# RWKV-7 time mixing on one core: where the k and r mixes are split, who makes the key norms' reciprocals, and which queue asks for the up weights

## The chip, the cores and the metric

The kernel runs on one core of a Trainium2 chip. The metric is the device time of one execution in microseconds (us). Before the change three runs gave 1647.22 us as median (1646.68 to 1648.98). One further execution was recorded by the profiler.

## What is computed

The reference is one layer of RWKV-7 time mixing with a residual, for 2048 tokens of width 1024 in 16 heads of 64. Each token's normalised input `h` is mixed with that of the token before it, once for each projection:

```python
dx = token_shift(h) - h
x_r, x_w, x_k, x_v, x_a, x_g = (h + dx * mu[i] for i in range(6))
r = x_r @ w_r;  k = x_k @ w_k;  v = x_v @ w_v;  g = silu(x_g @ w_g)
w_lo = tanh(x_w @ w_lo_w);  a_lo = x_a @ w_lo_a
decay = exp(-exp(-softplus(-(w0 + w_lo @ w_up)) - 0.5));  a = sigmoid(a0 + a_lo @ a_up)
kk = normalised per head (k * k_k);  k = k * (1 + (a - 1) * k_a)
# per token and head: S = S * decay + (S @ -kk) (kk * a)^T + v k^T;  y = S r
y = group_norm(y) + sum(r * k * r_k) * v
out = x + (y * g) @ w_out
```

All of it is in float32.

## The kernel before

A product of two float32 matrices is made of three matmuls. Each factor is split into a high part (the value rounded to the matmul's own 32-bit format, `fp32r`) and a low part (what is left), and the three products high x high, high x low and low x high are summed in PSUM. `split` (line 95) does this: ScalarE copies the value into the high part, another engine, VectorE as a rule, subtracts that from the value to get the low part. So each mix and each weight costs one ScalarE copy and one subtraction before TensorE can use it.

The work has three stages. The tokens are cut into 8 blocks of 256 (`NB`, index `b`), the width into 8 slices of 128 (`NCT`, index `ct`).

The first stage (lines 542 to 653, up to 477 us) runs over the blocks. For each slice it loads the input, makes `h` and `dx`, feeds the low-rank product `lps`, and makes four mixes. The mix for v goes into the tiles `mixa` (high and low) and the one for g into `mixb`; both are split there. The mixes for k and r (`mok`, `mor`, tag `mo`) are stored to DRAM unsplit, in `mkr_d`. In block 0 ScalarE and GpSimd make those two, in the others VectorE does. Then come the v product (two groups of columns by two groups of 128 tokens, so four PSUM sums, with three PSUM buffers of the tag `vg`) and the g product (eight sums over the same three buffers). `mixa` and `mixb` exist once, so a slice of them is written for the next block only when the product of this block has read it. The tiles `x`, `h`, `dx` and `mo` have two buffers each. In this stage a scheduler lays out the order of all engines' instructions from its own estimates; the order is then fixed.

The second stage (lines 655 to 1078, 477 to 1142 us) has an order written out by hand (`manual_schedule`) for TensorE, VectorE, ScalarE and GpSimd. `first_k` makes the k product of block 0. Then `step(b, p)` runs for each block and each of eight groups of 128 columns (`p`): it makes the r product of block `b` (`r_proj`, from `mixa`) and the k product of block `b + 1` (`k_proj`, from `mixb`), and the elementwise chains around them (`chain_a`, `chain_b`, `chain_c`). The mixes come back from DRAM by `load_mix`: the k mixes of block `b + 2` are asked for at `p == 6`, when `mixb` has been read, the r mixes of block `b + 1` at the end of `p == 7`. `load_mix` loads the raw mix into the low tile and returns eight steps, each of which splits one slice; `take(mixes, ...)` puts the steps into the order at `p == 7` and at `p == 0`. Every second subtraction goes to GpSimd.

Three more things of this stage matter here. The key norms: `rs_a` (at `p == 7`) turns sums of squares into reciprocal roots by `rsqrt` (line 99), eleven small instructions on VectorE; `rs_b` (at the next `p == 0`, after one `k_proj`) transposes the result on TensorE (`ssp<-consts,rsk`). The up weights: `load_up(p + 1)` asks for the next 128 KB of `up_d` on SyncE's queue, right after the matmuls of `chain_a` (tile `wa`) have read the single buffer `up`. And the queue: nearly all DMAs are issued by SyncE (SP), in the order in which they stand, each after the waits of the one before it.

The last block's step (`last`) and the third stage (from line 1190, 1142 us on) run the recurrence over chunks of 32 tokens with the output projection; none of the edited lines is there. The weights `w_out` pass through two of the `mkr_d` buffers in the meantime (`wo_d`).

Of the kernel before, what the change touches and what calls it, by code (L numbers as in the profile page):

```python
# [39 lines left out]
def rwkv7_kernel(ctx, tc, a, T):  # L40
# [45 lines left out]
    up_d = dram.tile([NP, P, 2, P], F32, name="up_d")  # L86
    mkr_d = [dram.tile([P, 2, NCT, TB], F32, name=f"mkr_d{b}") for b in range(NB)]
    bn_d = [dram.tile([2, P, HEADS], F32, name=f"bn_d{b}") for b in range(NB)]

    wo_d = lambda p: mkr_d[2 + p // 4].rearrange("p k c t -> p (k c t)")[:, p % 4 * D : p % 4 * D + D]  # L90
    pl_d = [dram.tile([P, NC, NP], F32, name=f"pl_d{b}") for b in range(NB)]
# [6 lines left out]

    def rsqrt(pool, out, x, shape, nm):

        y = pool.tile(shape, F32, name=nm + "y", tag="rq", bufs=3)
        t = pool.tile(shape, F32, name=nm + "t", tag="rq", bufs=3)
        h = pool.tile(shape, F32, name=nm + "h", tag="rq", bufs=3)
        ts(y.bitcast(I32), x.bitcast(I32), -0.5, 1597463007.0, mul, add)
        ts(h, x, -0.5, None, mul)
        for it in range(3):
            tt(t, y, y, mul)
            tt(t, t, h, mul)
            stt(y if it < 2 else out, t, 1.5, y, add, mul)

# [65 lines left out]

    def load_mix(k, mix, b, pool=False, n=NCT // 2):

        hi, lo = mix
        for x in range(0, NCT, n):  # L180
            nc.sync.dma_start(lo[:, x : x + n].bitcast(F32), mkr_d[b][:, k, x : x + n])

        def step(x):
            raw = lo[:, x].bitcast(F32)
            nc.scalar.copy(hi[:, x], raw)
            (nc.gpsimd if pool and x % 2 else nc.vector).tensor_tensor(out=lo[:, x], in0=raw, in1=hi[:, x].bitcast(F32), op=sub)  # L186

        return [lambda x=x: step(x) for x in range(NCT)]

# [314 lines left out]
    with ExitStack() as p0:  # L504
# [37 lines left out]
        with ExitStack() as pa:  # L542
# [48 lines left out]
            for b in range(NB):  # L591
                (mvh, mvl), (mgh, mgl) = mixa, mixb
                lps = pps.tile([P, TB], F32, name=f"lps{b}", tag="lps", bufs=1)
                for ct in range(NCT):
# [12 lines left out]
                    for i, nm in enumerate("kr"):  # L607
                        mo = hp.tile([P, TB], F32, name=f"mo{nm}{b}{ct}", tag="mo")
                        if b == 0:
                            act(mo, dx, AF.Copy, scale=pr("mu_" + nm, ct))  # L610
                            nc.gpsimd.tensor_tensor(out=mo, in0=mo, in1=h, op=add)
                        else:
                            stt(mo, dx, pr("mu_" + nm, ct), h, mul, add)
                        nc.sync.dma_start(mkr_d[b][:, i, ct], mo)
                    stt(dx, dx, pr("mu_g", ct), h, mul, add)
# [29 lines left out]
                if b == NB - 1:  # L645
                    wk, steps = load_w(a["w_k"], "wk", stage)
                    do(steps)
                    do(load_mix(0, mixa, 0))
                for i in range(NCT):
# [5 lines left out]
        with ExitStack() as pb:  # L655
# [73 lines left out]
            def rs_a(b):  # L729
                tr = tokenmajor(st["ssc"], st["ss", b])  # L730
                ss = sm.tile([P, 2, 16], F32, name=f"ss{b}", tag="ss", bufs=2)
                with urgent():
                    ts(ss.rearrange("p q (j x) -> p q j x", x=4), tr, 2.0, 2e-24, mul, ALU.max)
                    rs = sm.tile([P, 2, 16], F32, name=f"rsk{b}", tag="ss", bufs=2)
                    rsqrt(sm, rs, ss, [P, 2, 16], f"rk{b}")
                st["rs", b] = rs
# [46 lines left out]
            def load_up(p):  # L783
                up = sm.tile([P, 2, P], F32R, name=f"up{p}", tag="up")
                st.setdefault("up", deque()).append(up)
                nc.sync.dma_start(up.bitcast(F32), up_d[p % NP])

            def chain_a(b, p):
# [10 lines left out]
                for j in range(2):  # L799
                    nc.tensor.matmul(wup[j], up[:, j], x[:, j], start=True, stop=False)  # L800
                    nc.tensor.matmul(wup[j], up[:, j], x[:, 2 + j], start=False, stop=True)  # L801
                load_up(p + 1)
                th = t_("th")
                act(th, wup[0], AF.Tanh, scale=0.5, bias=dprm[:, 0, p : p + 1])
                act(th, th, AF.Identity, scale=C, bias=cb)
                yield
                nc.vector.tensor_tensor_scan(th, rmask.rearrange("p c l -> p (c l)"), th, 0.0, mul, add)
# [127 lines left out]
            def step(b, p):  # L935
# [21 lines left out]
                if p == 2 and b > 0:  # L957
                    bn_out(b - 1)
                if first:
                    take(mixes, 3 if b else 0)  # L960
                else:
                    take(inv, INA[p])
# [5 lines left out]
                if first:  # L968
                    rs_b(b)
                    prod_t()  # L970
                    take(mixes, NCT)
                    k_next()
# [23 lines left out]
                if final:  # L996
                    rs_a(b + 1)
                    take(mixes, 0 if last_mix else NCT)
                else:
                    next(ga, None)  # L1000
                    next(ga, None)
                if p == 6:
                    if b + 2 < NB:
                        mixes.extend(load_mix(0, mixb, b + 2, True))
                    else:
                        mixes.extend(load_mix(1, mixb, NB - 1, True))
                if not final:
# [26 lines left out]
            def first_k():  # L1034

                for p in range(NP):
# [4 lines left out]
                    next(kn[0], None)  # L1041
                    take(mixes, NCT // 4)
                    do(st["wr"], p / NP, (p + 1) / NP)
# [4 lines left out]
                st["ssc"] = save(st["ss", 0], 0, "ss")  # L1048
                mixes.extend(load_mix(1, mixa, 0, True))
                ga = chain_a(0, 0)  # L1050
# [5 lines left out]
            with tc.manual_schedule(engines=MANUAL):  # L1056
                mixes = deque(load_mix(0, mixb, 1, True))
                load_up(0)
# [17 lines left out]
                def last():  # L1076
# [6 lines left out]
                    load_c(2)  # L1083
                    take(mixes, NCT)
                    for _ in range(3):
# [238 lines left out]
```

## Time and profile before

| | |
|---|---|
| median of three runs | 1647.22 us |
| the profiled execution | 1646.02 us, span in the profile 1644.2 us |
| granted TensorE clock, mean | 0.978 of 2.4 GHz |
| busy: TensorE, VectorE, ScalarE, GpSimd | 1507.0, 1190.7, 835.9, 358.0 us |
| TensorE in the first stage, 82 to 477 us | busy for 387.99 of 395 us |
| DMA | 269.03 MB, mean 164 GB/s |

An engine's busy time is the union of its instructions. A matmul's end is modelled and overlaps the start of the next, so what TensorE really issues is read from the distance between starts. In a list of waits, "idle" is the time just before an instruction, and the name behind the arrow is what ended it. PE is TensorE, DVE VectorE, ACT ScalarE, POOL GpSimd, SP SyncE, and SPq its DMA queue.

### The profile page before, as it was taken

The page shows a single profiled execution, that of the slowest core. Times are in us where ns is not written, and L with a number is a line of the kernel's source. Part 1 is how long each engine was busy: PE and PEld are TensorE (multiplying, and loading weights), DVE is VectorE, ACT ScalarE, POOL GpSimd, SP SyncE. Part 2 cuts the span into 40 slices and gives each one's busy share as a digit, 9 for nine tenths or more (in the row PEclk, how much of TensorE's full clock was granted, in tenths as well). Part 3 has the DMA queues.
Part 4 walks back from the last instruction along what each step waited for, and adds up shares of the span by engine and source line. Part 5 has one row for each costly group of instructions (what it writes and reads, how often), then busy time and mean ns, then how long its engine had stood idle before and what let it go on. Part 6 is the DMA issues. An engine that isn't in the chain of part 4 may idle for free. (4 is left out here: it accounts for less than half of the span.)

```text
span 1644.2 us, 46239 instructions
## 1 busy us (share of the span) xinstructions
PE 1507.0 (92%) x17776; PEld 1304.6 (79%) x17776; DVE 1190.7 (72%) x2900; ACT 835.9 (51%) x2126; POOL 358.0 (22%) x729
## 2 busy tenths in 40 slices
PE   3699999999989999989998989698899999999998
PEld 2589889999888888878787878687677787777776
DVE  7976776668655579787878778578568867876654
ACT  5653332223356455454546454477566666666551
POOL 4600000000002232222313232312233222323221
PEclk9899999999999999999999999799899999999999
DMA  5783433334574565556576666778866687677642
GB/s 178 223 263 126 145 119 112 127 126 154 149 224 113 139 138 152 120 151 151 148 160 159 139 168 150 205 205 238 203 184 177 184 193 205 179 189 185 177 108 81
DMA packets 447389, 269.03 MB, mean 164 GB/s; under 512 B 304544, under 2 KB 387744, under 8 KB 447168
## 3 DMA queue, kind: packets, MB, share of 16 engines
q1 hardware_dynamic: 445824, 261.54, 59.2%
q10 hardware_dynamic: 1344, 4.52, 1.0%
q8 instruction: 141, 2.31, 0.6%
q14 instruction: 80, 0.66, 0.1%
HBM read 158.61 MB, written 111.54 MB: 164 GB/s over the span
## 5 line engine op out<-in xcount | busy, mean ns | idle before, releaser
L540 PE MATMUL gps<-mixbh,wgh 128*128 128x256 f32 x512 | 145.9, 285 | 4.6 <-ACT vo L635 4.5
L254 ACT COPY misc<-ybank 32x256 f32<-32x256 f32 x220 | 79.6, 362 | 130.1 <-PE ybank L249 126.7
L540 PE MATMUL gps<-mixbh,wgl 128*128 128x256 f32 x512 | 145.6, 284 | 0.0
L540 PE MATMUL gps<-mixbl,wgh 128*128 128x256 f32 x512 | 145.5, 284 | 0.0
L540 PE MATMUL kps<-mixbl,wkh 128*128 128x256 f32 x448 | 128.9, 288 | 16.0 <-DVE mixbl L186 16.0
L849 PE MATMUL rps<-mixah,wrh 128*128 128x256 f32 x448 | 135.2, 302 | 2.2 <-ACT sq L60 2.2
L51 DVE TENSOR_TENSOR x<-dp,misc 64x256 f32<-64x256 f32 x216 | 91.2, 422 | 62.2 <-PE dp L274 56.7
L540 PE MATMUL kps<-mixbh,wkh 128*128 128x256 f32 x448 | 132.8, 296 | 0.6 <-DVE u L48 0.6
L222 POOL MEMSET x<- 32x512 f32 x128 | 66.4, 519 | 299.6 <-PE ybank L289 231.1
L849 PE MATMUL rps<-mixal,wrh 128*128 128x256 f32 x448 | 129.2, 288 | 0.0
L849 PE MATMUL rps<-mixah,wrl 128*128 128x256 f32 x448 | 128.9, 288 | 0.0
L540 PE MATMUL kps<-mixbh,wkl 128*128 128x256 f32 x448 | 128.1, 286 | 0.0
L60 ACT ACTIVATE th<-wa,dprm 128x256 f32<-128x256 f32 x64 | 30.5, 476 | 172.4 <-PE wa L801 80.2
L249 PEld LDWEIGHTS ybank<-x,stat 128*64 128x64 f32 x1760 | 65.1, 139 | 58.3 <-issue 33.8
L540 PE MATMUL vps<-wvh,mixah 128*128 128x512 f32 x256 | 104.3, 407 | 5.6 <-ACT mixah L96 4.2
L460 PE MATMUL ops<-woh,oh 128*128 128x512 f32 x256 | 108.0, 422 | 0.0
L460 PE MATMUL ops<-woh,ol 128*128 128x512 f32 x256 | 106.4, 416 | 0.0
L460 PE MATMUL ops<-wol,oh 128*128 128x512 f32 x256 | 104.2, 407 | 0.0
L540 PEld LDWEIGHTS gps<-mixbh,wgh 128*128 128x128 f32 x512 | 98.9, 193 | 5.4 <-ACT vo L635 5.4
L540 PE MATMUL vps<-wvl,mixah 128*128 128x512 f32 x256 | 101.8, 398 | 0.0
L540 PEld LDWEIGHTS kps<-mixbl,wkh 128*128 128x128 f32 x448 | 87.3, 195 | 17.2 <-DVE mixbl L186 17.2
L297 ACT COPY y<-ybank 32x256 f32<-32x256 f32 x220 | 80.0, 364 | 37.6 <-PE ybank L289 35.5
(326 smaller groups left out, 4578.1 us busy)
## 6 DMA issues: line engine op xcount, KB each, us to landing
stat<-sm_d SPq DMA_DIRECT2D x64, 512.0 KB, 5.0
dk<-bt_d SPq DMA_DIRECT2D x128, 128.0 KB, 4.6
sm_d<-ra SPq DMA_DIRECT2D x112, 128.0 KB, 3.1
sm_d<-mo SPq DMA_DIRECT2D x224, 64.0 KB, 2.2
bt_d<-bo SPq DMA_DIRECT2D x56, 256.0 KB, 3.3
up<-up_d SPq DMA_DIRECT2D x65, 128.0 KB, 2.6
xn<-x SPq DMA_DIRECT2D x32, 256.0 KB, 4.7
mkr_d<-mok SPq DMA_DIRECT2D x64, 128.0 KB, 2.0
```

Of the source, the lines that this page charges most:

```text
L51: return nc.vector.tensor_tensor(out=out, in0=in0, in1=in1, op=op)
L60: nc.scalar.activation(out, in_, f, **k)
L222: nc.gpsimd.memset(x[bu(h), h], 0.0)
L249: nc.tensor.matmul(y[half(h), p], st[:, h, 4 * w + p], x[:, h, 4 * w + p], start=(p == 0), stop=(p == 3), tile_position=(0, 64 * h))
L254: nc.scalar.copy(gs[bu(h)], y[kv(h)])
L297: ev(2, h)(ys[t][o : o + L, c // 2, 4 * w : 4 * w + 4], bank[w][bu(h), ch % 2])
L460: nc.tensor.matmul(ps, l[:, ct], r(ct, ns), start=(ct == 0 and k == 0), stop=(ct == NCT - 1 and k == 2))
L540: nc.tensor.matmul(ps, x, y, start=first, stop=last)
L849: nc.tensor.matmul(ps, x, y, start=first, stop=last)
```

## The change

The mixes for k and r are split in the first stage, by the same `split` as the others, and both parts are stored: `mkr_d` gets one more axis of two. The tag `mo` gets three buffers, which the unsplit mix (later its low part, in place) and its high part share. `load_mix` loads the high and low parts straight into their tiles and has no steps any more, so all `take(mixes, ...)` go. The added loads stand in SP's queue where the old ones stood, twice as many of the same size. `rsqrt` gets an engine; for the key norms it is GpSimd, which does the nine instructions of the three rounds in twelve, since the fused step becomes two. `load_up` asks on ScalarE's queue, after the two activations that follow the matmuls.

```diff
-    mkr_d = [dram.tile([P, 2, NCT, TB], F32, name=f"mkr_d{b}") for b in range(NB)]
+    mkr_d = [dram.tile([P, 2, 2, NCT, TB], F32, name=f"mkr_d{b}") for b in range(NB)]
...
-    def rsqrt(pool, out, x, shape, nm):
+    def rsqrt(pool, out, x, shape, nm, e=nc.vector):
...
-            tt(t, y, y, mul)
-            tt(t, t, h, mul)
-            stt(y if it < 2 else out, t, 1.5, y, add, mul)
+            e.tensor_tensor(out=t, in0=y, in1=y, op=mul)
+            e.tensor_tensor(out=t, in0=t, in1=h, op=mul)
+            if e is nc.vector:
+                stt(y if it < 2 else out, t, 1.5, y, add, mul)
+            else:
+                e.tensor_scalar(out=t, in0=t, scalar1=1.5, scalar2=None, op0=add)
+                e.tensor_tensor(out=y if it < 2 else out, in0=t, in1=y, op=mul)
...
-    def load_mix(k, mix, b, pool=False, n=NCT // 2):
-
-        hi, lo = mix
+    def load_mix(k, mix, b, n=NCT // 2):
+
         for x in range(0, NCT, n):
-            nc.sync.dma_start(lo[:, x : x + n].bitcast(F32), mkr_d[b][:, k, x : x + n])
-
-        def step(x):
-            raw = lo[:, x].bitcast(F32)
-            nc.scalar.copy(hi[:, x], raw)
-            (nc.gpsimd if pool and x % 2 else nc.vector).tensor_tensor(out=lo[:, x], in0=raw, in1=hi[:, x].bitcast(F32), op=sub)
-
-        return [lambda x=x: step(x) for x in range(NCT)]
+            for i in range(2):
+                nc.sync.dma_start(mix[i][:, x : x + n].bitcast(F32), mkr_d[b][:, k, i, x : x + n])
...
-                        mo = hp.tile([P, TB], F32, name=f"mo{nm}{b}{ct}", tag="mo")
+                        mo = hp.tile([P, TB], F32, name=f"mo{nm}{b}{ct}", tag="mo", bufs=3)
...
-                        nc.sync.dma_start(mkr_d[b][:, i, ct], mo)
+                        mh = hp.tile([P, TB], F32R, name=f"mh{nm}{b}{ct}", tag="mo", bufs=3)
+                        split(mh, mo.bitcast(F32R), mo)
+                        nc.sync.dma_start(mkr_d[b][:, i, 0, ct], mh.bitcast(F32))
+                        nc.sync.dma_start(mkr_d[b][:, i, 1, ct], mo)
...
-                    rsqrt(sm, rs, ss, [P, 2, 16], f"rk{b}")
+                    rsqrt(sm, rs, ss, [P, 2, 16], f"rk{b}", nc.gpsimd)
...
-                nc.sync.dma_start(up.bitcast(F32), up_d[p % NP])
+                nc.scalar.dma_start(up.bitcast(F32), up_d[p % NP])
...
-                load_up(p + 1)
                 th = t_("th")
                 act(th, wup[0], AF.Tanh, scale=0.5, bias=dprm[:, 0, p : p + 1])
                 act(th, th, AF.Identity, scale=C, bias=cb)
+                load_up(p + 1)
...
-                    take(mixes, NCT)
...
-                    if b + 2 < NB:
-                        mixes.extend(load_mix(0, mixb, b + 2, True))
-                    else:
-                        mixes.extend(load_mix(1, mixb, NB - 1, True))
+                    load_mix(*((0, mixb, b + 2) if b + 2 < NB else (1, mixb, NB - 1)))
...
-                        mixes.extend(load_mix(1, mixa, b + 1, True, 2))
+                        load_mix(1, mixa, b + 1, 2)
```

## Rows read from the trace of the kernel before

**Rows 1.** The page's first part: busy us (share of the span) and instructions.

```profile
PE 1507.0 (92%) x17776; PEld 1304.6 (79%) x17776; DVE 1190.7 (72%) x2900; ACT 835.9 (51%) x2126; POOL 358.0 (22%) x729
```

**Rows 2.** Busy time by stretches, us: the first stage after its start.

```profile
82.00:477.00 395.00, 387.99 (x2561) 354.33 (x2562) 279.77 (x768) 138.46 (x353) 3.87 (x8) 1.00 0.46 152
```

**Rows 3.** The same view; stretch, us, PE, PEld, DVE, ACT, POOL, PEclk, DMA, GB/s.

```profile
191.40:213.60 22.20, 22.20 (x187) 22.20 (x186) 7.89 (x19) 4.42 (x12) 0.00 (x0) 1.00 0.38 131
213.60:239.50 25.90, 25.71 (x137) 21.62 (x136) 24.10 (x65) 9.85 (x27) 0.00 (x0) 1.00 0.39 127
```

**Rows 4.** Instructions of VectorE in time order: start us, us, line, operation.

```profile
233.60 0.42 DVE L97 TENSOR_TENSOR hl<-ha,hh 128x257 fp32r<-128x257 f32 x1
233.94 0.48 DVE L48 SCALAR_TENSOR_TENSOR mor<-dxa,prm,ha 128x256 f32<-128x256 f32 x1
...
234.73 0.42 DVE L97 TENSOR_TENSOR mixal<-xa,mixah 128x256 fp32r<-128x256 f32 x1
...
238.82 0.41 DVE L97 TENSOR_TENSOR mixbl<-dxa,mixbh 128x256 fp32r<-128x256 f32 x1
```

**Rows 5.** TensorE in time order: start of g, last v slice, next g.

```profile
191.44 0.29 PE L540 MATMUL gps<-mixbh,wgh 128*128 128x256 f32 x1
...
235.54 0.63 PE L540 MATMUL vps<-wvh,mixal 128*128 128x512 f32 x2
...
243.57 0.29 PE L540 MATMUL gps<-mixbh,wgh 128*128 128x256 f32 x1
```

**Rows 6.** Groups of instructions: busy us, mean ns, idle before.

```profile
L96 ACT CAST mixah<-xa 128x256 fp32r<-128x256 f32 x64 | 25.8, 405 | 32.9 <-DVE xa L48 22.0 <-issue 6.6 <-PE vps L540 4.2
```

**Rows 7.** DMA issues: count, KB each, median us to landing.

```profile
mkr_d<-mok SPq DMA_DIRECT2D x64, 128.0 KB, 2.0
```

**Rows 8.** Busy time by stretches: block 0 of the first stage.

```profile
25.00:82.00 57.00, 39.58 (x154) 29.79 (x154) 55.69 (x85) 35.61 (x82) 33.62 (x37) 0.91 0.70 211
```

**Rows 9.** Waits of TensorE: us in total, times, longest us.

```profile
PE kps L540 <- DVE mixbl L186: 16.0, 6, 3.4
PE wa L800 <- DMA up<-up_d: 9.6, 10, 1.6
...
PE mps L899 <- ACT ta L60: 4.1, 1, 4.1
...
PE rps L849 <- ACT sq L60: 2.2, 1, 2.2
```

**Rows 10.** Busy time by stretches: from the k load to its use, block 1.

```profile
641.00:652.50 11.50, 9.88 (x93) 8.77 (x91) 10.87 (x25) 9.60 (x26) 5.42 (x9) 0.85 0.83 211
```

**Rows 11.** SyncE's DMA queue in time order: an up request, a k load.

```profile
600.58 1.60 SPq L786 DMA_DIRECT2D up<-up_d  x1
...
641.15 1.98 SPq L181 DMA_DIRECT2D mixbl<-mkr_d  x2
```

**Rows 12.** ScalarE in time order: r weights in block 0, splits in block 7.

```profile
485.78 0.62 ACT L96 CAST wrh<-wrs 128x512 fp32r<-128x512 f32 x1 [4.22 <-DMA wrs<-w_r]
...
1047.13 2.55 ACT L185 CAST mixbh<-mixbl 128x256 fp32r<-128x256 f32 x8
```

**Rows 13.** VectorE in time order: last step before the rounds, two blocks.

```profile
508.22 0.17 DVE L55 TENSOR_SCALAR rk0h<-ss 128x32 f32<-128x32 f32 x1
...
649.79 0.75 DVE L55 TENSOR_SCALAR rk2h<-ss 128x32 f32<-128x32 f32 x1
```

**Rows 14.** The chain that ended last: three rounds on GpSimd, first and last.

```profile
1611.81 0.18 POOL m L383
...
1615.19 0.23 POOL rst L383
```

**Rows 15.** TensorE in time order: transpose of the reciprocals, first k product.

```profile
510.52 0.38 PE L742 MATMUL ssp<-consts,rsk 128*16 128x128 f32 x2
...
652.04 0.28 PE L849 MATMUL rps<-mixah,wrl 128*128 128x256 f32 x1
652.16 0.28 PE L540 MATMUL kps<-mixbh,wkh 128*128 128x256 f32 x1
```

More of the change, by code (lines that the diff above doesn't have):

```diff
@@ L86, in rwkv7_kernel @@
     up_d = dram.tile([NP, P, 2, P], F32, name="up_d")
-    mkr_d = [dram.tile([P, 2, NCT, TB], F32, name=f"mkr_d{b}") for b in range(NB)]
+    mkr_d = [dram.tile([P, 2, 2, NCT, TB], F32, name=f"mkr_d{b}") for b in range(NB)]
     bn_d = [dram.tile([2, P, HEADS], F32, name=f"bn_d{b}") for b in range(NB)]
-    wo_d = lambda p: mkr_d[2 + p // 4].rearrange("p k c t -> p (k c t)")[:, p % 4 * D : p % 4 * D + D]
+    wo_d = lambda p: mkr_d[2 + p // 4].rearrange("p k l c t -> p (k l c t)")[:, p % 4 * D : p % 4 * D + D]
     pl_d = [dram.tile([P, NC, NP], F32, name=f"pl_d{b}") for b in range(NB)]
@@ L647, in rwkv7_kernel @@
                     do(steps)
-                    do(load_mix(0, mixa, 0))
+                    load_mix(0, mixa, 0)
                 for i in range(NCT):
@@ L958, in step @@
                     bn_out(b - 1)
-                if first:
-                    take(mixes, 3 if b else 0)
-                else:
+                if not first:
                     take(inv, INA[p])
@@ L997, in step @@
                     rs_a(b + 1)
-                    take(mixes, 0 if last_mix else NCT)
                 else:
@@ L1002, in step @@
                 if p == 6:
-                    if b + 2 < NB:
-                        mixes.extend(load_mix(0, mixb, b + 2, True))
-                    else:
-                        mixes.extend(load_mix(1, mixb, NB - 1, True))
+                    load_mix(*((0, mixb, b + 2) if b + 2 < NB else (1, mixb, NB - 1)))
                 if not final:
@@ L1041, in first_k @@
                     next(kn[0], None)
-                    take(mixes, NCT // 4)
                     do(st["wr"], p / NP, (p + 1) / NP)
@@ L1048, in first_k @@
                 st["ssc"] = save(st["ss", 0], 0, "ss")
-                mixes.extend(load_mix(1, mixa, 0, True))
+                load_mix(1, mixa, 0)
                 ga = chain_a(0, 0)
@@ L1056, in rwkv7_kernel @@
             with tc.manual_schedule(engines=MANUAL):
-                mixes = deque(load_mix(0, mixb, 1, True))
+                load_mix(0, mixb, 1)
                 load_up(0)
@@ L1083, in last @@
                     load_c(2)
-                    take(mixes, NCT)
                     for _ in range(3):
```

## The prediction, written before the result was known

> **What bounds the kernel now.** I read the busy times of the page first, then the stretches by stage, then the order of work inside one stage, and last the waits of TensorE. The page gives TensorE 92% of the span [rows 1], so time is lost only where it waits, and saved only where a wait of its ends. In the first stage (blocks of v and g projections, 82 to 477 us) TensorE is busy for 388 of 395 us [rows 2]. The average of VectorE there, 71%, hides two unlike halves [rows 3]: in the 22.2 us of the g products it works for 7.9 us, in the 25.9 us in which the mixes of the next block are made it works for 24.1 us. In that second half both engines are full. The order inside it shows which leads: VectorE ends the v mix of the last slice (mixal) at 234.73 + 0.42 = 235.15 us, TensorE takes it at 235.54, and g begins at 243.57 [rows 4, 5]. So TensorE has nothing in reserve when that mix arrives. What it does afterwards is fixed: the rest of the three open v sums, then the fourth sum, which has no PSUM buffer before, 8.4 us in all. Whatever delays mixal of slice 7 delays g. In the second stage (blocks of k and r, 510 to 1046 us) TensorE's named waits are 16.0 us for k mixes still being split (6 waits), 9.6 us for up weights (10), 4.1 us and 2.2 us [rows 9]. The third stage, the recurrence after 1142 us, holds none of the edited code.
>
> **What the change adds in the first stage.** Per block 8 slices x 2 mixes get one ScalarE copy, one VectorE subtraction and one more DMA: 128 of each.
>
> Subtractions, blocks 1 to 7: of the 16 per block, those of slices 0 and 1 fall into the idle half; the 12 of slices 2 to 7 fall into the full one. A subtraction of this shape takes 0.34 us of VectorE from start to start (233.60 to 233.94) [rows 4]. Ten of the 12 must come before mixal of slice 7, the last two can follow it; I take 11: 3.7 us. They can't be put off into the idle half: each leaves its buffer only once it is written to DRAM, three buffers hold one and a half mixes, and h and dx have two each. The bounds per block are 0 (the idle 1.8 us of the window and a better order swallow them) and 12 x 0.42 = 5.0 (no overlap of starts). 7 x 3.7 = 26.
>
> Buffers of tag mo: before, a mix had one of two buffers. Now a mix needs two of three, and the high part of a mix waits until that of the mix before it has landed: one copy 0.405 us [rows 6] and one landing 2.0 us [rows 7], 2.4 us a mix. Twelve mixes so need 29 us, where the half that holds them is 25.9 us long [rows 3] and becomes 29.6 by the subtractions alone. The two limits lie close together, and g's own last mix (mixbl of slice 7, written at 238.82 [rows 4]) has 4 us to spare before g begins. The second limit adds 0 to 7 us a block (a rival below); I take 0.5, nearest to the landing in the row: 3.5 in all.
>
> Block 0: from 25 to 82 us VectorE is busy for 55.7 of 57 us while TensorE is busy for 39.6 [rows 8], so 16 x 0.34 = 5.4 us go straight into the start of g. Bounds 0 and 8.
>
> The ScalarE copies hide in an engine that works 9.85 of 25.9 us [rows 3]; uncovered they would add 0.8 us a slice. The 16.8 MB more of writes find the DMA engines 39% busy there. First stage: 26 + 3.5 + 5.4 = **+35 us**.
>
> **What it takes from the second stage.**
>
> Wait for the k mixes, 16.0 us in 6 blocks [rows 9]: the splits go, and the load is late next. It doubles to 2 MB. In block 1 it is asked for at 641.15 [rows 11] and TensorE wants it at 652.16 [rows 15], the second half 1.4 us later. In that stretch the DMA engines are 83% busy at 211 GB/s [rows 10]: they have 2 us free of 11.5, while the extra megabyte takes 4.1 us at the rate that fully busy engines would give (211 / 0.83 = 254 GB/s). So the tail comes up to 2 us late or pushes other transfers. I give back 1 us a block (bounds 0 and 2.7): -16 + 6 = -10.
>
> Up weights, 9.6 us: SP asks for them when its queue comes to them, as at 600.58 [rows 11], behind loads of others. On ScalarE's queue they are asked for after the second activation on the matmul's result. The ten waits are 1 us each, and that request alone stood 1.6 us in SP's queue. -8 (bounds -9.6 and 0; the request costs ScalarE some 0.5 us a time, hidden while it is half idle).
>
> r mixes of block 0, -2.2 (bounds -2.2 and 0). In the last block ScalarE's eight copies, 2.55 us at 1047.13 [rows 12], stand before the activation that TensorE waits 4.1 us for [rows 9]: -2.5 (bounds -2.5 and 0).
>
> At the head of this stage the doubled k load of block 1 stands before the r weights in SP's queue. ScalarE already waits 4.2 us for these until 485.78 [rows 12], with TensorE's copies behind it. The extra megabyte costs between 1.8 us (two more requests; two took 1.98 [rows 11]) and 4.1; I take +3.5.
>
> Reciprocals on GpSimd: two of the steps stay on VectorE, nine become twelve. The same twelve at half the width run from 1611.81 to 1615.42 on GpSimd, 3.6 us [rows 14]; with twice the width some 4.0. In block 0 they begin at 508.4 [rows 13] and end near 512.5, against 510.52 where TensorE now uses them [rows 15]: +2. In blocks 1 to 6 the steps before them end near 650 (649.79 [rows 13], with less GpSimd work beside it), so the result comes at 654.1; without the k wait TensorE wants it after one k product, its 24 matmuls at 0.12 us (652.04 to 652.16) [rows 15] after 652.16, at 655. 0.9 us to spare, no cost. The row of the GpSimd chain gives 0.3 us a step. The Trainium skill (GPSIMD Engine Reference, section 8, Key points) holds elementwise work on VectorE to be structurally about twice as fast; by that, an estimate from VectorE's 0.19 us doubled, the chain would take 5.4 us, the 0.9 us would be gone, and the sum would come out some 4 us higher.
>
> SP spends 2 us more a block on the two added requests, with stores of products behind them, and saves 0.5 on each up request: +2 in all (bounds -3 and +6).
>
> Second stage: -10 - 8 - 2.2 - 2.5 + 3.5 + 2 + 2 = **-15 us** (bounds -30 and -2).
>
> **Sum.** The profiled execution took 1646.0 us, 1.8 us over its span and 1.2 us under the median of the runs. 1646.0 + 35 - 15 = 1666; at the level of the median 1667 us. Per cent: 1.2% slower.
>
> **Rivals.**
>
> Faster, the first stage swallows the subtractions. For it: VectorE has 14 us idle in each g half, and the scheduler, which lays out this stage by its own order, may put the work there. Against: the buffers above bind it to the full half. It decides at (15 - 5.4) / 7 = 1.4 us of delay per block; below that the kernel gains. With 2 us in all: 1647 + 2 - 15 = 1634 us.
>
> Even: the delay per block is near 1.4 us, because part of the subtractions fall into VectorE's 1.8 us of idle time and after mixal of slice 7: 1647 us, within 3.3 us (0.2%, what a measurement of this kernel tells from no change).
>
> Slower still: landings of the doubled writes take 2.4 in place of 2.0 us, a mix 2.8; twelve then end at 249 and g begins at 250.5, 7 us late: 49 + 8 - 15 = +42, 1689 us. For it: VectorE waits for these buffers now and then already. Against: the DMA engines are 39% busy.
>
> The change doesn't do what it says: the doubled k load comes so late that a DMA wait takes the place of the whole 16.0 us: +10, 1677 us.
>
> **How the numbers follow.** Forecast 0.45 (1655 to 1678 by its own bounds), late loads 0.06, slower still 0.15, even 0.10, faster 0.24. So slower by over 0.2% 0.66, within 0.2% 0.10, faster 0.24. The range 1631 to 1690 leaves out the better half of the faster case and the worse part of the slowest.
>
> **What would show it.** Right: from one start of g to the next it takes about 56 us, where it is 52.1 now (191.44 to 243.57) [rows 5], with TensorE idle in the full half for VectorE; the row of TensorE's waits for mixbl and for up goes; the second stage shortens by about 2 us a block; the new GpSimd chain ends before its transpose except in block 0. Wrong: the starts of g keep their 52 us (then the kernel is faster), or TensorE waits for the mix load at each block of the second.

## The result, and the profile of the changed kernel

The changed kernel takes 1715.42 us (median of 4 runs, 1710.13 to 1721.26). Beside the kernel before this is a ratio of 1.042, interval 1.039 to 1.044: slower, as forecast, but outside the range given (1631 to 1690). The profiled execution took 1712.95 us with a span of 1711.2, 67 us more than the span before. One more run of the kernel before, of 2772.42 us, is left out of the ratio and of the median above.

The first part of the page of the changed kernel (busy us, share of the span, instructions; before: [rows 1]):

```profile
PE 1530.3 (89%) x17776; PEld 1320.8 (77%) x17776; DVE 1180.3 (69%) x2888; ACT 843.1 (49%) x2126; POOL 338.6 (20%) x765
```

TensorE's share fell by three points, so it waits more. Where, is told by three moments that can be read off TensorE's time order in both traces: the first g product, the first k product (end of the first stage) and the first `ybank` matmul (taken here as the start of the third, 1151.6 us before the change; its first lines begin at 1142). The third stage is counted to the last matmul. I cut the second stage at the `rsk` transposes of block 0 and block 7 as well. In us:

| | before | after | change | forecast |
|---|---|---|---|---|
| block 0, up to its g | 82.1 | 94.6 | +12.5 | +5.4 |
| rest of the first stage, to the first k product | 395.1 | 442.6 | +47.5 | +29.5 |
| second stage: head, to `rsk` of block 0 | 33.4 | 40.3 | +6.9 | |
| seven blocks, `rsk` to `rsk` | 534.0 | 527.5 | -6.5 | |
| last block | 107.0 | 116.6 | +9.6 | |
| second stage in all | 674.4 | 684.4 | +10 | -15 |
| third stage | 488.9 | 486.0 | -3 | 0 |

The same stretches by busy time, after (columns as in [rows 3]; the first answers to [rows 2]):

```profile
94.60:537.20 442.60, 401.45 (x2562) 360.29 (x2561) 316.36 (x840) 168.77 (x440) 4.50 (x9) 0.98 0.50 166
537.20:1221.60 684.40, 612.30 (x7163) 548.09 (x7161) 456.01 (x1116) 335.60 (x794) 160.11 (x379) 0.95 0.71 181
```

and the second stage of the kernel before:

```profile
477.10:1151.60 674.50, 608.86 (x7163) 542.64 (x7162) 508.75 (x1248) 369.32 (x914) 179.63 (x343) 0.97 0.65 160
```

In the first stage TensorE, busy for all but 7 of 395 us before, now stands idle for 41 of 443. In the second, VectorE lost 53 us of work and ScalarE 34, and the stage is longer all the same; the DMA engines' share rose from 0.65 to 0.71. What TensorE waits for in the changed kernel (us in total, times, longest; before: [rows 9]):

```profile
PE vps L537 <- ACT mixah L96: 35.4, 25, 2.3
...
PE ssp L742 <- POOL e L816: 17.6, 7, 4.2
...
PE tps L870 <- DVE mo L51: 11.8, 7, 3.0
PE mps L899 <- ACT bo L873: 9.8, 1, 9.8
...
PE wa L800 <- DMA up<-up_d: 0.5, 1, 0.5
```

The two waits that the change aimed at are gone (k mixes 16.0, up weights 9.6 to 0.5). Two new ones stand in their place (`ssp` and `mps` for `bo`), and two have grown (`vps` for `mixah` from 4.2 us, `tps` for `mo` from 4.8). The first of the list is the first stage's: TensorE waits 25 times for the high part of a v mix from ScalarE. One such place, the queue, VectorE, ScalarE and TensorE in time order:

```profile
315.21 0.32 SPq L613 DMA_DIRECT2D mkr_d<-mhk  x1
...
316.37 0.48 DVE L48 SCALAR_TENSOR_TENSOR mor<-dxa,prm,ha 128x256 f32<-128x256 f32 x1 [0.73 <-DMA mkr_d<-mor]
317.04 0.41 ACT L96 CAST mhr<-mor 128x256 fp32r<-128x256 f32 x1 [1.86 <-DMA mkr_d<-mhk]
...
317.36 0.40 ACT L96 CAST mixah<-xa 128x256 fp32r<-128x256 f32 x1
...
317.81 0.79 PE L537 MATMUL vps<-wvh,mixah 128*128 128x512 f32 x1 [2.02 <-ACT mixah L96]
```

The k mix's high part is stored at 315.21. The copy of the r mix's high part needs that buffer, and ScalarE, idle for 1.86 us, begins it when that store has landed. (The r mix itself was ready only at 316.85, 0.2 us earlier: VectorE had to wait for a buffer as well.) ScalarE works in order, so the copy of the next slice's v mix, 0.3 us behind it, waits too, and TensorE is idle for 2.02 us. ScalarE's own list has such a wait 50 times, 63.6 us in all; in 20.4 us of them, by the time order, VectorE had not yet made the mix:

```profile
ACT mhr L96 <- DMA mkr_d<-mhk: 44.2, 29, 2.7
...
ACT misc L251 <- DMA misc<-bn_d: 20.2, 1, 20.2
...
ACT mhk L96 <- DMA mkr_d<-mhr: 19.4, 21, 2.7
```

The second row is one wait of 20.2 us in the last block (`rsk` to third stage, 1105 to 1222). In time order:

```profile
1093.07 0.51 ACT L60 ACTIVATE th<-th,cb 128x256 f32<-128x256 f32 x1
1113.43 0.33 ACTq L786 DMA_DIRECT2D up<-up_d  x1
1113.80 0.74 ACT L251 COPY misc<-yb 32x256 f32<-32x256 f32 x2 [20.22 <-DMA misc<-bn_d]
1114.56 0.58 ACT L873 COPY bo<-tps 128x512 f32<-128x512 f32 x1
...
1115.20 0.48 PE L899 MATMUL mps<-ra,bk 64*64 64x64 f32 x4 [9.82 <-ACT bo L873]
```

Between the activation and everything behind it stands the request for up weights. It leaves only at 1113.43, and TensorE is idle for 9.82 us.

The GpSimd chain in block 2 (its list entry is named after `e`, the next GpSimd instruction, but the matmul reads `rsk`):

```profile
712.80 0.76 DVE L51 TENSOR_TENSOR mo<-mps,consts 128x256 f32<-128x256 f32 x2 [1.60 <-DMA sm_d<-mo]
...
713.78 0.17 DVE L55 TENSOR_SCALAR rk2h<-ss 128x32 f32<-128x32 f32 x1
...
713.95 0.63 POOL L107 TENSOR_TENSOR rk2t<-rk2y 128x32 f32<-128x32 f32 x1 [3.03 <-DVE rk2h L55]
...
718.10 0.25 POOL L113 TENSOR_TENSOR rsk<-rk2t,rk2y 128x32 f32<-128x32 f32 x1
...
718.41 0.39 PE L742 MATMUL ssp<-consts,rsk 128*16 128x128 f32 x2 [0.90 <-POOL e L816]
```

Twelve steps take 713.95 to 718.35, 4.4 us. They start late because VectorE, in order, stood behind a small product `mo` that waited for a buffer whose store had not landed.

### The profile page after: what moved, and what is told of

The parts are those of the page before. It is cut to its first block, busy times and chain, and to the rows that moved or that the text cites. A ratio compares the mean times of both kernels' runs of the same rounds, so it can differ in the third digit from the quotient of the medians.

```text
span 1711.2 us, 46603 instructions
## 1 busy us (share of the span) xinstructions
PE 1530.3 (89%) x17776; PEld 1320.8 (77%) x17776; DVE 1180.3 (69%) x2888; ACT 843.1 (49%) x2126; POOL 338.6 (20%) x765
## 5 line engine op out<-in xcount | busy, mean ns | idle before, releaser
L537 PE MATMUL vps<-wvh,mixah 128*128 128x512 f32 x256 | 111.0, 433 | 35.9 <-ACT mixah L96 35.4
L537 PE MATMUL vps<-wvl,mixah 128*128 128x512 f32 x256 | 107.4, 420 | 0.0
L537 PEld LDWEIGHTS gps<-mixbl,wgh 128*128 128x128 f32 x512 | 98.1, 192 | 1.0 <-DVE mixbl L97 0.9
```

Of the source, the lines that this page charges most:

```text
L537: nc.tensor.matmul(ps, x, y, start=first, stop=last)
```

## Experiments

Each was profiled; ratios are to runs of the kernel before on the same chip (medians 1641.9 to 1644.1; for the changed kernel the three runs of 1647.22). The stage figures come from TensorE's time order as above, each from one execution. "A block" is the mean distance of g's starts over the last six distances.

| kernel | us | ratio, interval | first g | a block | first k | second stage: head, seven, last |
|---|---|---|---|---|---|---|
| before | | | 82.1 | 51.7 | 477.1 | 674.4: 33.4, 534.0, 107.0 |
| after | 1715.4 | 1.042, 1.039 to 1.044 | 94.6 | 59.5 | 537.2 | 684.4: 40.3, 527.5, 116.6 |
| e1_no_sub | 1674.6 | 1.019, 1.011 to 1.027 | 84.7 | 54.7 | 498.7 | 691.1: 38.9, 533.2, 119.1 |
| e2_bufs2 | 1758.5 | 1.070, 1.064 to 1.076 | 116.0 | 62.2 | 582.0 | 684.6: 40.3, 529.7, 114.6 |
| e3_bufs5 | 1690.9 | 1.029, 1.022 to 1.036 | 80.7 | 55.0 | 509.4 | 692.5: 40.0, 533.9, 118.7 |
| e10_b5_no_sub | 1673.4 | 1.019, 1.016 to 1.021 | 79.8 | 53.1 | 493.8 | 688.6: 39.3, 533.3, 116.0 |
| e8_b5_pool | 1684.2 | 1.027, 1.025 to 1.029 | 81.0 | 56.6 | 518.8 | 671.8: 37.3, 522.1, 112.3 |
| e4_split_only | 1705.8 | 1.038, 1.032 to 1.044 | 94.1 | 59.6 | 540.3 | 678.4: 36.8, 530.6, 111.0 |
| e7_half_loads | 1682.4 | 1.025, 1.024 to 1.027 | 92.6 | 59.5 | 538.1 | 650.1: 34.0, 507.8, 108.3 |
| e9_few_bytes | 1684.3 | 1.025, 1.022 to 1.027 | 94.2 | 59.1 | 538.8 | 654.7: 33.2, 514.3, 107.2 |
| e11_rs_back | 1709.3 | 1.041, 1.039 to 1.043 | 92.6 | 59.8 | 535.8 | 686.8: 38.0, 531.6, 117.2 |
| e5_up_only | 1660.6 | 1.012, 1.010 to 1.014 | 82.3 | 51.9 | 475.1 | 692.1: 36.3, 539.4, 116.4 |
| e6_rs_only | 1650.6 | 1.006, 1.004 to 1.008 | 81.4 | 52.0 | 479.0 | 680.3: 35.2, 536.5, 108.5 |
| e12_dve_split | 1643.1 | 1.000, 0.998 to 1.001 | 82.2 | 51.9 | 476.9 | 674.8: 33.0, 534.7, 107.1 |

The table also shows how far one execution can be trusted. Five rows have the same second stage (after, e1, e2, e3, e10: the edits are in the first), and it takes 684.4 to 692.5 us; e4 and e8 share another, 678.4 and 671.8. So a difference of less than some 8 us between two second stages is not told from none.

**The first stage.** Theory: two causes, VectorE's subtractions (as forecast) and the wait for a buffer on ScalarE, in order. The first takes the subtractions away, on the changed kernel:

```diff
-split(mh, mo.bitcast(F32R), mo)
+nc.scalar.copy(mh, mo)
```

> Leaves out the subtraction that makes the low part of the k and r mixes: the unsplit mix is stored in its place, all copies, buffers and DMAs stay. Theory A (the 128 added subtractions on VectorE set the first stage): that stage ends some 31 us earlier than after the change (k product of block 0 starts near 506 us in place of 537), total near 1683. Theory B (each high part waits on ScalarE for one of three buffers until an earlier mix has landed in DRAM, and the v mixes stand behind it): the buffers come free at most 0.5 us earlier a mix, so the stage gives back 5 to 15 us, total 1700 to 1710.

A block falls from 59.5 to 54.7 us, block 0 by 9.9, and the stage ends 38.5 us earlier, more than theory A's 31. The wait `vps<-mixah` falls from 35.4 to 4.0 us. This run alone can't part the two theories: a mix that needs no subtraction is also stored sooner, so its buffer comes free sooner.

Next the buffers: two, then five (five need room, so a fourth staging tile for weights goes).

```diff
-tag="mo", bufs=3
+tag="mo", bufs=2      # e2_bufs2
+tag="mo", bufs=5      # e3_bufs5, with stager(sp, 512, 3) for stager(sp, 512, 4)
```

> The tag mo gets two buffers in place of three, nothing else changes. Theory A: VectorE has the same work, nothing moves by more than 5 us. Theory B: a mix can't be begun before both parts of the mix before it have landed; a mix takes about 0.5 + 0.4 + 0.4 + 2.2 = 3.5 us, twelve 42 us in place of 30, so 7 to 12 us more in each of 7 blocks: first stage 50 to 85 us longer, total 1765 to 1800.

> The tag mo gets five buffers in place of three; the room for them comes from the staging tiles of the first stage, three in place of four. Theory A: nothing gained, total 1713 plus what the missing staging tile costs at the start (0 to 5 us). Theory B: copies no longer wait for landings, a block of the first stage goes from 59.5 to 52 to 55 us (what is left is VectorE's subtractions), 30 to 50 us back: total 1665 to 1685.

One buffer fewer costs 21.4 us in block 0 and 2.7 us a block after it (theory B had 7 to 12); two more bring block 0 to 80.7 us, under the kernel before, and a block to 55.0, the end of theory B's 52 to 55 (its total, 1690.9 us, is above theory B's 1685). (After the first g there are 74.5 us to the next where the changed kernel has 59.8. With a staging tile fewer the last g weights land at 90.0 us, 72.6 in the changed kernel; this happens once, and that the staging tile is its whole cause was not tested.) Either cure takes away most of block 0's 12.5 us: five buffers all of it, no subtractions 9.9. With two buffers ScalarE's wait, and with it TensorE's, is at its largest, and VectorE waits for buffers too (50.4 us, 42 times); the upper fence is ScalarE, the lower TensorE:

```profile
ACT mhr L96 <- DMA mkr_d<-mok: 58.1, 28, 3.7
```

```profile
PE lps L599 <- ACT hh L96: 49.4, 21, 6.7
```

Both cures at once, to see whether the causes are two:

```diff
-split(mh, mo.bitcast(F32R), mo)
+nc.scalar.copy(mh, mo)      # with bufs=5 and stager(sp, 512, 3) as in e3_bufs5
```

> The changed kernel with five buffers for k and r mixes (three staging tiles in place of four) and without the subtractions of k and r in the first stage (their low part is left out). Alone, leaving out the subtractions brought a block from 59.5 to 55.3 us, and five buffers to 55.0. Theory A (two separate causes that add): 59.5 - 4.2 - 4.5 = 50.8, that is the kernel before's 52 us a block, for TensorE is the bound again. Theory B (one cause seen twice: either cure already leaves what TensorE, ScalarE's 11 more copies and the doubled stores allow): 54 to 55 us a block.

53.1 us a block. The cures bring 4.7 and 4.5 us alone and 6.4 together, of the 7.8 that the change costs: two causes, but they overlap (a copy that waits for a buffer also delays a subtraction, and the reverse), and neither theory's number was hit; 1.4 us a block stay unexplained.

A part of what the cures share is TensorE's clock. The last six distances in the changed kernel, in e1_no_sub and in e3_bufs5 (columns as in [rows 3]):

```profile
154.40:511.20 356.80, 323.27 (x2024) 289.04 (x2023) 252.25 (x652) 127.56 (x335) 3.87 (x8) 0.97 0.45 150
143.30:471.70 328.40, 316.61 (x2018) 281.09 (x2018) 216.07 (x551) 127.47 (x333) 3.88 (x8) 1.00 0.48 161
155.20:484.90 329.70, 315.64 (x2017) 280.83 (x2017) 246.13 (x658) 130.12 (x332) 3.85 (x8) 1.00 0.48 161
```

Each cure gives back 27 to 28 us here: about 20 are idle time of TensorE, and 7 are shorter busy time on the same matmuls, with the granted clock back at 1.00. Those 7 us can be given back only once.

A cure that keeps the result, on the split alone: five buffers, and the subtractions of k and r on GpSimd, which is idle in this stage.

```diff
-split(mh, mo.bitcast(F32R), mo)
+split(mh, mo.bitcast(F32R), mo, nc.gpsimd if b else None)   # with bufs=5, stager(sp, 512, 3)
```

> The split and direct loads of the change, reciprocals on VectorE and up weights on SyncE's queue as before, with five buffers for k and r mixes (three staging tiles in place of four) and the low-part subtractions of k and r on GpSimd after block 0. Theory A (the first stage has two causes that add: 11 subtractions of 0.34 us on VectorE and the in-order wait for buffers on ScalarE): with both taken away the blocks after the second come to 52 to 53 us against 59.5, the k product of block 0 starts near 500 us, and the whole is about 1670 us. Theory B (GpSimd's subtractions are slower, share VectorE's port, or the stores behind them land later): blocks of 55 us or more, as with five buffers alone, and a total at or above 1685 us. Either way it stays over the kernel before.

56.6 us a block, worse than with five buffers and the subtractions on VectorE (55.0). Groups of instructions from 213 us to the end of the stage (busy us, mean ns, idle before), this kernel:

```profile
L48 DVE SCALAR_TENSOR_TENSOR dxa<-dxa,prm,ha 128x256 f32<-128x256 f32 x39 | 32.6, 836 | 0.2
L48 DVE SCALAR_TENSOR_TENSOR mor<-dxa,prm,ha 128x256 f32<-128x256 f32 x39 | 25.3, 648 | 1.7 <-DMA mkr_d<-mok 1.7
...
L97 POOL TENSOR_TENSOR mok<-mok,mhk 128x256 fp32r<-128x256 f32 x39 | 36.7, 941 | 171.1 <-ACT mhk L96 171.1
```

and the changed kernel:

```profile
L48 DVE SCALAR_TENSOR_TENSOR mor<-dxa,prm,ha 128x256 f32<-128x256 f32 x40 | 19.3, 484 | 7.2 <-DMA mkr_d<-mor 7.0
L48 DVE SCALAR_TENSOR_TENSOR dxa<-dxa,prm,ha 128x256 f32<-128x256 f32 x40 | 19.3, 482 | 0.2
...
L97 DVE TENSOR_TENSOR mok<-mok,mhk 128x256 fp32r<-128x256 f32 x40 | 17.0, 425 | 6.9 <-ACT mhk L96 6.7
```

A subtraction takes GpSimd 941 ns in place of 425, and two of VectorE's own operations beside it go from 482 to 836 ns and from 484 to 648; with five buffers and the subtractions on VectorE (e3_bufs5) both take 482 to 483. What was to be taken off VectorE came back as longer instructions.

**The second stage.** First the split and the direct loads without the other two edits:

```diff
-rsqrt(sm, rs, ss, [P, 2, 16], f"rk{b}", nc.gpsimd)
-nc.scalar.dma_start(up.bitcast(F32), up_d[p % NP])   # and load_up(p + 1) back behind the matmuls
+rsqrt(sm, rs, ss, [P, 2, 16], f"rk{b}")
+nc.sync.dma_start(up.bitcast(F32), up_d[p % NP])
```

> The split of the mixes as changed, but reciprocals on VectorE and up weights asked for on SyncE's queue as before. Theory C (in the second stage the GpSimd chain of 4.6 us and the up request on ScalarE, which waits for DMAs of other queues, cost what the removed splits gained): first stage unchanged at 537 us, TensorE's waits of 17.6 us for the reciprocals and 9.8 us in the last block go, the 9.6 us for up weights come back: second stage 15 to 20 us shorter than after, total near 1695. Theory D (the doubled loads in SyncE's queue are what costs in the second stage): total within 5 us of after.

Neither theory's number: the second stage is 678.4 us, 6 us shorter than after, and the whole 1705.8. The stage is no shorter than before (674.4), though it has lost every split, so the loads themselves are the suspect. In the next kernel each mix is loaded by half, so that as many bytes move as before the change:

```diff
-for i in range(2):
+for i in range(1):
     nc.sync.dma_start(mix[i][:, x : x + n].bitcast(F32), mkr_d[b][:, k, i, x : x + n])
```

> The split and the direct loads of the change, with reciprocals on VectorE and up weights on SyncE's queue as before (its full form took 1705.8 us), but only the high part of each mix is loaded: the low part's tile keeps what it held, so the low products are wrong. The second stage's mix loads are then as many bytes as in the kernel before and half as many requests. Theory A (the doubled bytes and requests take back the second stage's gain: late stores, late mo, k products that wait): second stage 678 -> about 664 us, the waits tps<-mo (9.9) and wa<-mo (6.7) fall to the kernel before's 4.8 and 4 or less; total about 1692. Theory B (the loads are hidden, the second stage is held by VectorE's u and ra and by a lower granted clock): second stage within 3 us of 678, total about 1703.

650.1 us: 24.3 less than before, 28.3 less than with both halves (21.7 less than the second stage of e8_b5_pool, which loads both halves too). So the doubled loads take the gain back. The second stage with both halves and with one:

```profile
540.30:1218.70 678.40, 614.25 (x7162) 547.99 (x7161) 470.96 (x1188) 332.25 (x794) 134.03 (x281) 0.95 0.72 183
538.10:1188.30 650.20, 602.39 (x7163) 539.68 (x7162) 471.20 (x1188) 332.63 (x794) 133.94 (x282) 0.97 0.67 166
```

TensorE's idle time makes 16 us of the difference; the other 12 are longer busy time on the same matmuls, at a lower granted clock. Half of the expectation failed, and in an instructive place: `tps<-mo` and `wa<-mo` stayed as they were (10.1 and 6.7), but the k product's wait, which the profile puts down to VectorE's `u`, fell from 13.7 us to 3.1. VectorE's waits for stores of `mo` go the same way, with both halves (upper fence) and with one:

```profile
DVE mo L51 <- DMA sm_d<-mo: 35.8, 10, 7.5
```

```profile
DVE mo L51 <- DMA sm_d<-mo: 16.9, 4, 5.7
```

Of the 224 stores of `mo` 46 take over 4 us to land with both halves, 27 with one and 29 before the change. VectorE stands at the border of the blocks behind a store that lands late, and `u`, the reciprocals and the k product's buffer are behind it. That these waits set the stage's length is read from the order and was not tested; e8_b5_pool has 38.4 us of them in a stage of 671.8.

Bytes or requests? All requests are made, but those for low parts bring one channel tile each:

```diff
+m = n if i == 0 else 1
-nc.sync.dma_start(mix[i][:, x : x + n] ..., mkr_d[b][:, k, i, x : x + n])
+nc.sync.dma_start(mix[i][:, x : x + m] ..., mkr_d[b][:, k, i, x : x + m])
```

> The split and direct loads alone (full form: 1705.8 us, second stage 678.4; high part only: 1682.4 us, second stage 650.2). Here every request of the full form is made, but each request for a low part brings one channel tile of 2 or 4 (the rest of the low tile keeps what it held, so the low products are wrong): 1.25 times the kernel before's bytes where the halves are of 4 tiles, 1.5 times where they are of 2. Theory A (the number of requests in SyncE's queue, in order ahead of the small stores of mo and ra, is what costs): second stage stays within 6 us of 678. Theory B (the bytes cost: landings of 6 us and late stores under a busy share of 0.9 and more): second stage about 650 + 0.3 x 28 = 658 us. Between 664 and 670 both count.

654.7 us, near theory B's 658: the bytes. That it is 4.6 us longer than e7_half_loads, with all the requests and some more bytes, is within the scatter of one execution.

The up weights by themselves, on the kernel before:

```diff
-nc.sync.dma_start(up.bitcast(F32), up_d[p % NP])
+nc.scalar.dma_start(up.bitcast(F32), up_d[p % NP])    # and load_up(p + 1) behind the second act
```

> The kernel before with one edit: the up weights are requested on ScalarE's queue, after the two activations. Theory A (the prediction's term, -8 us): the waits wa<-up (9.6 us before) go and nothing takes their place: about 1637 us against 1642 to 1648, ratio 0.995. Theory B (the request on ScalarE itself waits for transfers of SyncE's queue): in the last block ScalarE stands behind one request for 10 to 20 us, as in the changed kernel, where an ACT wait of 20.2 us and a TensorE wait mps<-bo of 9.8 us are listed: gain in blocks 1 to 6 of about 8, loss in block 7 of about 10: ratio 1.000 to 1.003, with a single long ACT wait in the trace. If no such ACT wait shows here, the stall belongs to the doubled mix loads and not to the request.

Slower by 1.2%, more than either theory: TensorE's waits for up fell to 1.1 us (0.42 and 0.71), but those of `tps` for `mo` rose from 4.8 to 14.4, and the last block is 9.4 us longer. One border of blocks in time order:

```profile
681.73 0.51 ACT L60 ACTIVATE th<-th,cb 128x256 f32<-128x256 f32 x1
...
685.52 0.33 ACTq L786 DMA_DIRECT2D up<-up_d  x1
...
685.95 0.37 ACT L706 COPY k<-kps 128x256 f32<-128x256 f32 x1 [3.71 <-DMA z<-sm_d]
```

ScalarE had nothing to wait for but the request, and the request left when a load of `z`, issued on SyncE's queue, had landed: ScalarE lost 3.7 us here, and 17.3 us in one piece in the last block. The stall needs no doubled mix loads.

What ties the request to that load is in the trace, which holds the semaphores that each instruction waits for. (A semaphore is a counter; here a DMA's landing raises it.) The landings of all DMAs of this program are told by eight semaphores, which the requests of SyncE and ScalarE share. Before the request leaves, ScalarE waits until the semaphore that the request is to use has been raised by the DMA that used it last:

| request leaves | its semaphore | used last by SyncE's | which landed |
|---|---|---|---|
| 685.52 (e5_up_only) | 105 | `z<-sm_d` | 685.50 |
| 1056.87 (e5_up_only, last block) | 102 | `misc<-pl_d` | 1056.81 |
| 1113.43 (after, last block) | 106 | `dk<-bt_d` | 1113.37 |

So in these three places the request is held by a semaphore that the two queues share. A version in which it has a semaphore of its own was not run.

The reciprocals by themselves, on the kernel before:

```diff
-rsqrt(sm, rs, ss, [P, 2, 16], f"rk{b}")
+rsqrt(sm, rs, ss, [P, 2, 16], f"rk{b}", nc.gpsimd)
```

> The kernel before with one edit: the iterations of the key norms' reciprocals on GpSimd. Theory A (the prediction's term, +2 us): the chain takes 4 us in place of 2 but has 0.9 us to spare in blocks 1 to 6, so only block 0 is longer; ratio 1.001. Theory B (from the changed trace, where TensorE waits 17.6 us for the chain in 7 blocks, 0.9 to 4.25 us each): the chain takes 4.4 to 4.6 us and ends after the k product in every block, whatever the mix loads are: 7 x about 1.5 to 2.5 us, +10 to +17 us, ratio 1.006 to 1.010. Theory C (the wait belongs to the late start of the chain that the doubled loads cause): the k product of this kernel still waits for mixbl as before (16.0 us), the chain runs beside that wait and little shows: ratio 1.000 to 1.003.

Slower by 0.6%, theory B by its size but not by its place. In this kernel GpSimd still makes every second subtraction of the k mixes, the chain stands before them in its order, and the wait of 16.0 us grows:

```profile
PE kps L544 <- POOL mixbl L190: 23.2, 6, 4.3
```

Then the same edit undone in the changed kernel (`rsqrt` on VectorE, all else as changed):

> The changed kernel with the reciprocals back on VectorE (split, direct loads, up weights on ScalarE's queue as changed). Alone on the kernel before, GpSimd's chain cost 9.5 us and up weights on ScalarE's queue 19 us; the split alone cost 63; the whole change 68, not 91. Theory A (behind the doubled loads the chain on GpSimd costs its listed wait of 17.6 us): about 1698 us. Theory B (taking the chain off VectorE gives back nearly what the wait costs once the loads are late, as the sum suggests): within 5 us of the changed kernel, 1710 to 1718 us. Theory C (it is the request on ScalarE that costs less behind the doubled loads): the chain still costs about 9, so about 1706 us, and the up weights no more than 5.

Theory B, though the median of 1709.3 us is just under its range: 1.041 against 1.042, second stage 686.8 against 684.4. TensorE's row of 17.6 us for the chain is gone, and this one has come (it is not in the changed kernel's list):

```profile
PE kps L537 <- DVE u L48: 12.2, 6, 2.6
```

The 17.6 us were the last of several waits that ended close together, and taking it away gained nothing that can be told from scatter.

Last, on the kernel before, a version that might beat both: every subtraction of the second stage on VectorE, because VectorE's 28 subtractions for r in that stage take 746 ns at the median beside GpSimd's, and 418 to 422 where it works alone.

```diff
-load_mix(..., True)
+load_mix(...)          # pool=False everywhere
```

> The kernel before with one edit: every subtraction of the mixes in the second stage on VectorE, none on GpSimd (before, every other one). In the kernel before VectorE's r subtractions take 746 ns at the median beside GpSimd's of 828, against 419 for the k subtractions; in the run with GpSimd subtractions in the first stage VectorE's own operations went from 482 to 836 ns beside them. Theory A (two engines at once are no faster than VectorE alone): the k product's wait (16.0 us) stays within 4 us, r's subtractions take 8 x 0.34 = 2.7 us a block in place of about 3; ratio 0.995 to 1.000, a little faster than the kernel before. Theory B (VectorE is the scarce engine at the border of the blocks, and 4 more subtractions there and 4 more for r, 8 x 0.34 = 2.7 us a block, put u, ra and the scan later): ratio 1.003 to 1.010.

No difference (0.998 to 1.001). VectorE's r subtractions take 418 ns now, but there are twice as many, and the k product waits 6.1 us for `mixbl` and now 10.1 us for `u`, 16.2 in place of 16.0. No version here beats the kernel before.

## Why the prediction was wrong

The direction was right, and so was the frame: TensorE leads in the first stage, the third is untouched, 67 = 60 + 10 - 3. Both sums in the middle failed, each by some 25 us.

**First stage, +60 for +35.** The step that failed is the sentence on the buffers of tag `mo`: "I take 0.5, nearest to the landing in the row". It compared two totals, 29 us of copies and landings against a half block of 29.6, as if the waits could move within it. They can't: each holds up whatever ScalarE has next, and that is the copy for TensorE. With it failed "the ScalarE copies hide in an engine that works 9.85 of 25.9 us": little work is no proof that a copy is done in time, and TensorE's wait for ScalarE's v mixes went from 4.2 to 35.4 us. The rival "slower still" had the buffers as the limit and about their size (7 us a block), but by a total again and with the wrong trigger: landings needn't be longer, their medians were 1.9 to 2.4 us.

What the two terms measured depends on each other. The subtractions are worth 4.7 us a block with three buffers and 1.9 with five (55.0 less 53.1), the buffers 4.5 with the subtractions and 1.6 without (54.7 less 53.1); the forecast had 3.7 and 0.5. In block 0 it had 5.4 for the subtractions alone: 9.9 of the 12.5 us go when they are left out, but with five buffers they cost 0.9 (80.7 less 79.8). So the term for the subtractions is near the measured one only by where it falls between the two. The sum also has no term for TensorE's clock, which fell to 0.97 in the last six distances.

**Second stage, +10 for -15.** The profiled runs form a chain in which one edit is added at a time:

| step | second stage | change | forecast |
|---|---|---|---|
| before | 674.4 | | |
| no splits, direct loads, bytes as before (e7) | 650.1 | -24.3 | -20.7 |
| both halves loaded (e4) | 678.4 | +28.3 | +11.5 |
| up weights on ScalarE's queue (e11) | 686.8 | +8.4 | -8 |
| reciprocals on GpSimd (after) | 684.4 | -2.4 | +2 |

(-20.7 is 16 + 2.2 + 2.5; +11.5 is 6 + 3.5 + 2.) The first two changes stand clear of the scatter of some 8 us; the third is at its edge, the last within it. The gain from the splits was there, and not smaller than forecast. Two steps failed. "I give back 1 us a block" looked for the price of a megabyte where the k product reads it, and asked whether the load is in time. It was in time: TensorE's list has no wait of the k product for a load. Late were small stores issued beside it, and VectorE behind them; and TensorE's busy time grew by 12 us at a lower clock. The rival "doesn't do what it says" named the loads but the same wrong place. And "the request costs ScalarE some 0.5 us a time" counted the issue and not the waits that a request brings with it: the rows for up went, as forecast, but 6.2 of the +8.4 us lie in the last block, where ScalarE's one long stall is, and on the kernel before the edit alone costs 17.7 us in the second stage. The stated bounds of -30 and -2 are no help either: the upper bounds of the terms, as given, add up to +12 and not to -2, and the measured +10 lies inside them.

**Reciprocals.** "0.9 us to spare" failed in all six blocks of which it was said (15.4 us of waits), since VectorE's part of the chain ended later: in block 2 at 713.95, 0.5 us before the first k product (714.47), where the forecast had 2.2 us (650 and 652.16), with the `mo` wait of 1.60 just before. In block 0 the wait was 2.2 us for +2. The change is within the scatter, as the forecast of next to nothing was, but for another reason: the next wait was as long. The duration, 4.0 us estimated from the narrow chain, was 4.4. The Trainium skill (GPSIMD Engine Reference, section 8, Key points) has VectorE about twice as fast on elementwise work; here the twelve starts on GpSimd lie 0.38 us apart (718.10 less 713.95, by 11), VectorE's in e4_split_only, below, 0.22, so the factor is 1.7, near the page. The forecast's estimate by the Trainium skill does not come out as it is written: twelve steps of 0.19 us doubled are 4.6 us, not 5.4.

```profile
712.08 0.19 DVE L107 TENSOR_TENSOR rk2t<-rk2y 128x32 f32<-128x32 f32 x1
712.30 0.19 DVE L108 TENSOR_TENSOR rk2t<-rk2t,rk2h 128x32 f32<-128x32 f32 x1
```

**The signs named beforehand.** From g to g 59.5 us for 56, with TensorE idle for ScalarE where VectorE was named; the row for `mixbl` gone and that for up down to 0.5 us, right; the seven blocks shorter by 0.9 us each for 2; the GpSimd chain late in blocks 0 to 6.

Open: 1.4 us a block of the first stage, at a granted clock of 1.00 (e10_b5_no_sub), and how much of the second stage's loss each of the late stores and the lower clock would cost by itself.

## What to carry to other kernels

A buffer that comes free by a landing holds up its whole engine in order, so ask what stands behind the waiting instruction and not whether the waits fit into the stage's total. Before moving a request to another engine, ask what that engine will wait for before the request can leave. When a load is doubled, look for its price also at the small stores that land beside it, not only where it is read. A row of waits is worth what remains when the next one in line has taken its place: here a row of 17.6 us went away for no gain that shows (e11_rs_back), and 8.5 us of one row came back as 9.6 of another (e5_up_only).

## What the runs showed of the hardware

- A DMA request on ScalarE's queue stopped ScalarE for 3.7 us, 17.3 us and 20.2 us until transfers of another queue had landed, though its issue takes 0.33 us. In the three places of the table under e5_up_only the request left 0.02 to 0.06 us after the landing of the DMA that had used its semaphore last.
- VectorE operations with two inputs took 836 in place of 482 ns, and 648 in place of 484, beside GpSimd subtractions of 941 ns. The Trainium skill (GPSIMD Engine Reference, section 8, Key points) states that the two share their SBUF interfaces and contend where VectorE has two SBUF inputs; these rows agree. In the second stage GpSimd's share of the subtractions is worth nothing either way (e12_dve_split).
- The mean granted TensorE clock of the second stage was 0.97 before, 0.95 after and 0.97 with half the loads (a mean over stretches at 1.2 and at 2.4 GHz). It fell where TensorE had waited: in block 3 the stretch with the `ssp` wait of 4.25 us (5.75 of 10 us busy) has 0.90, and the next, full one still 0.93 (changed kernel, columns as in [rows 3]). So a new wait can cost a little more than its own length.

```profile
787.20:797.20 10.00, 5.75 (x42) 5.53 (x42) 4.30 (x13) 3.84 (x10) 4.36 (x15) 0.90 0.78 210
797.20:807.20 10.00, 10.00 (x101) 8.64 (x101) 6.13 (x16) 4.55 (x11) 1.96 (x4) 0.93 0.70 196
```
